# Own planned times for the first eight tiles of x, and whole projections copied to SBUF by ACT, in a hybrid attention block

## The chip, the cores and the metric

The kernel runs on one core of a Trainium2 chip. The metric is the device time of one execution in microseconds (us). Five engines work side by side, each through its own list of instructions, strictly in the order in which the program wrote them: PE (matmuls; PEld is its weight load), DVE (vector), ACT (activation), POOL, and SP, which here only issues DMAs. An instruction whose input is not there yet holds up everything behind it on its engine. Matmul results land in PSUM, in banks of 128x512 fp32.

## The reference, cut to what matters

```python
h = rms_norm(x, norm_gain)                      # x: 2048 x 1024, fp32
proj = h @ w_in                                 # q, k, v of mixers A and B; gates ga, gb; merge logits mg
qa = head_rms_norm(qa, q_norm_a) * scale;  ka = head_rms_norm(ka, k_norm_a)
ya, _ = banded_attention(qa, ka, va, A_WINDOW, 1, bias_a, sink_a)
ya = ya * silu(ga)
for g, (window, dilation) in enumerate(((128, 1), (512, 4), (2048, 16))):
    o, l = dilated_group(qb[:, :, g], kb[:, :, g], vb[:, :, g], window, dilation, bias_b[g])
yb = sum(softmax(stack(lses)) * stack(outs)) * silu(gb)
merged = sigmoid(mg_a + b) * (ya @ w_branch_a) + sigmoid(mg_b + b) * (yb @ w_branch_b)
y = x + merged @ w_out
```

## The kernel before

Precision comes from splitting: each fp32 operand of a matmul is a high and a low fp16 part, and a product is three matmuls (high by high, high by low, low by high). XH and XL are the parts of the normalised x, turned so that features lie on partitions; they stay in SBUF. A step named `hi` is ACT's conversion to fp16, a step `lo` is DVE's remainder after it.

There are three stages in time.

**Input stage.** x comes in 16 tiles of 128 rows, named t0 to t15 here. Each goes through: load (SP), sum of squares on ACT (L448), for a group of tiles together a first guess of 1/rms on DVE (L452, L261) and three Newton steps (12 small operations on POOL, L270 to L273, for groups of four; 9 on DVE, L275 to L277, for groups of two), a scaling on DVE (L462), then for each half of the features four transposes on PE (L468) into one of three PSUM banks "s", XH by ACT (L471) and XL by DVE (L475). T(t,h) is the group of four transposes of tile t, half h. The groups of tiles are (0,1), (2,3), (4..7), (8..11), (12..15). Beside this run projections of the gates: for gate block c (0 or 1) and quarter q of the rows (four tiles) a stream of 24 matmuls at L308, called c0q0, c1q0, c0q1 and so on. c0q0 needs tiles 0 to 3, and the split weights gh, gl of its block (raw weights graw, gain on POOL, norm, L350 and L354). At the start `warm` issues matmuls on constants.

**Units.** 14 units (a mixer's head group) of 8 pairs. A pair is two blocks of 128 rows: for each, the projection to q, k and v (24 matmuls at L651, or 48 where the rows of v are shifted against those of q and k) into one of two PSUM banks "pj". ACT copies q and k to the fp32 tile rw (evac_qk, L670), makes V's high part (v_hi, L685) from the same bank, DVE its low part (v_lo, L691). Then q and k are normalised: square (L698), sums and guess (L703, L704, L261), Newton on POOL, scale on DVE (L715), gain on POOL (L722), hi (L728), lo (L732), swap (L737), and a transposing DMA from SP (turn, L745) into kq, from which PE makes the logits (L805). Maxima (L820), exponentials (L828), their hi and lo (L833, L837), a turn (L843) and the values (L854) follow. Into eight units more gate projections are mixed, with a weight preparation: square of the raw gate weights on ACT (L332, which also gives gsq), and a small norm matmul on PE (L194).

**Tail.** Gates, branch projections, merge and output projection, nearly all of it PE work.

What sets the order is a table of numbers: a step is put into a heap with a planned time (`at(t, f)`, `chain` for steps that must follow each other), and `until(pos)` writes out all steps due before PE's planned position. These numbers decide the order of instructions and nothing else; on the chip only order, data and free buffers count. In the units time is counted in pairs: EVAC holds the delays of evac_qk, v_hi and v_lo after a projection, NORM those of the nine steps of the norm.

## Time and profile before

| | us |
|---|---|
| median of 3 runs (1957.21 to 1961.2) | 1960.59 |
| the profiled execution | 1960.34 |
| its span in the trace | 1958.6 |
| PE busy | 1935.7 |
| DVE busy | 1377.4 |
| ACT busy | 1059.8 |
| POOL busy | 956.0 |

The span runs from the first to the last recorded instruction; the time is 1.74 us longer than it. The input stage ends at about 81 us (first matmul of a unit's projection), the units at about 1449 us. A row of the timeline gives start, duration, engine, line, operation, output and inputs, and in brackets the idle time of the engine just before with what ended it. Matmuls are pipelined: the distance from one start to the next is what one costs, not its listed duration.

### The profile page before, as it was taken

The page shows a single profiled execution, that of the slowest core. Times are in us where ns is not written, and L with a number is a line of the kernel's source. Part 1 is how long each engine was busy: PE and PEld are TensorE (multiplying, and loading weights), DVE is VectorE, ACT ScalarE, POOL GpSimd, SP SyncE. Part 2 cuts the span into 40 slices and gives each one's busy share as a digit, 9 for nine tenths or more (in the row PEclk, how much of TensorE's full clock was granted, in tenths as well). Part 3 has the DMA queues.
Part 4 walks back from the last instruction along what each step waited for, and adds up shares of the span by engine and source line. Part 5 has one row for each costly group of instructions (what it writes and reads, how often), then busy time and mean ns, then how long its engine had stood idle before and what let it go on. Part 6 is the DMA issues. An engine that isn't in the chain of part 4 may idle for free.

```text
span 1958.6 us, 48091 instructions
## 1 busy us (share of the span) xinstructions
PE 1935.7 (99%) x17606; PEld 1392.0 (71%) x17606; DVE 1377.4 (70%) x3604; ACT 1059.8 (54%) x2415; POOL 956.0 (49%) x2440
## 2 busy tenths in 40 slices
PE   8999999999999999999999999999999999999999
PEld 5567896677788898888989889899544444444444
DVE  6668777888768776667876878767776757876312
ACT  7457656776565566565666655656534545432100
POOL 4254556455546656647566676656511210232533
PEclk8999999999999999999999999999999999999999
DMA  6239987797848596677777776755822346788763
GB/s 250 81 81 168 194 150 159 141 187 141 177 101 184 118 185 126 125 148 164 152 132 154 135 169 126 143 118 118 187 81 85 106 165 195 218 241 268 252 228 145
DMA packets 589773, 308.46 MB, mean 157 GB/s; under 512 B 458080, under 2 KB 527328, under 8 KB 588256
## 3 DMA queue, kind: packets, MB, share of 16 engines
q1 hardware_dynamic: 589536, 305.39, 67.0%
q8 instruction: 137, 2.24, 0.5%
q14 instruction: 100, 0.82, 0.1%
HBM read 129.91 MB, written 65.27 MB: 100 GB/s over the span
## 4 chain that ended last, share of the span: by engine, by line
PE 80%; DVE 6%; POOL 6%; issue 4%; ACT 2%; DMA 2%; SPq 0%; POOLq 0%; DVEq 0%; ACTq 0%
PE pj L651 32%; PE pj L308 14%; PE fps L308 13%; PE fps L1614 7%; PE fps L1409 5%; PE s L805 4%; PE pv L854 4%; POOL rs_t L270 1%; DVE rw L715 1%; POOL rs_t L271 1%; DVE qss L703 1%; POOL rs_t L272 1%; POOL rw L722 1%; POOL rs_y L273 1%; PE pt L916 1%
## 5 line engine op out<-in xcount | busy, mean ns | idle before, releaser
L651 PE MATMUL pj<-wl,XH 128*128 128x128 f16 (+2 forms) x2816 | 715.2, 268 | 0.0
L651 PE MATMUL pj<-wh,XH 128*128 128x128 f16 (+2 forms) x2816 | 708.7, 268 | 4.0 <-DVE vt L691 4.0
L651 PE MATMUL pj<-wh,XL 128*128 128x128 f16 (+2 forms) x2816 | 711.6, 269 | 0.0
L651 PEld LDWEIGHTS <-XH 128*128 128x128 f16 x5632 | 574.6, 113 | 64.7 <-issue 5.8
L651 PEld LDWEIGHTS <-XL 128*128 128x128 f16 x2816 | 318.1, 113 | 26.7 <-issue 0.5
L820 DVE CUSTOM_DVE_ANT_0 pr<-s,b,ubuf 128x256 f32<-128x256 f32 (+3 forms) x512 | 218.6, 464 | 48.6 <-PE s L805 47.0
L270 POOL TENSOR_TENSOR rs_t<-rs_y 128x8 f32<-128x8 f32 (+2 forms) x345 | 105.4, 306 | 207.5 <-DVE rs_y L261 142.7
L837 DVE SCALAR_TENSOR_TENSOR p<-pr,p 128x512 f16<-128x512 f32 (+2 forms) x256 | 185.0, 723 | 21.6 <-ACT p L833 21.1
L308 PEld LDWEIGHTS <-wh 128*128 128x128 f16 x960 | 93.7, 98 | 111.0 <-issue 1.5
L715 DVE TENSOR_TENSOR rw<-rw,qr 128x512 f32<-128x512 f32 (+1 forms) x112 | 111.6, 997 | 86.7 <-POOL vt L678 58.4
L722 POOL TENSOR_TENSOR rw<-rw,g 128x128 f32<-128x128 f32 (+1 forms) x224 | 131.1, 605 | 78.1 <-DVE rw L715 62.1
L833 ACT ACTIVATE p<-pr 128x512 f16<-128x512 f32 (+2 forms) x256 | 159.5, 623 | 7.1 <-issue 0.3
L670 ACT ACTIVATE rw<-pj 128x256 f32<-128x256 f32 (+1 forms) x224 | 86.5, 386 | 134.3 <-PE pj L651 133.4
L737 POOL COPY spl<-spl 128x256 f16<-128x256 f16 (+1 forms) x224 | 93.7, 448 | 127.2 <-DVE spl L732 125.7
L308 PE MATMUL fps<-Y,wh 128*128 128x512 f16 x512 | 152.2, 379 | 0.0
L805 PE MATMUL s<-kq 128*128 128x128 f16 (+1 forms) x1856 | 147.3, 218 | 1.5 <-DMA kq<-spl 1.4
L805 PEld LDWEIGHTS <-kq 128*128 128x128 f16 x2016 | 129.8, 98 | 25.1 <-issue 2.0
L308 PE MATMUL pj<-XH,gh 128*128 128x512 f16 x384 | 145.5, 379 | 0.0
L308 PE MATMUL pj<-XH,gl 128*128 128x512 f16 x384 | 145.5, 379 | 0.0
L308 PE MATMUL pj<-XL,gh 128*128 128x512 f16 x384 | 145.5, 379 | 0.0
L1614 PE MATMUL fps<-wt,M 128*128 128x512 f16 (+1 forms) x684 | 145.2, 375 | 0.0
L728 ACT ACTIVATE spl<-rw 128x512 f16<-128x512 f32 (+1 forms) x112 | 72.1, 644 | 126.2 <-POOL vt L678 87.0
(241 smaller groups left out, 3702.2 us busy)
## 6 DMA issues: line engine op xcount, KB each, us to landing
wraw<-in_w_units_dram SPq DMA_DIRECT2D x56, 384.0 KB, 4.6
mtd<-mm SPq DMA_DIRECT2D x56, 256.0 KB, 3.7
M<-mtd SPq DMA_DIRECT2D x8, 1792.0 KB, 9.5
mgd<-fg SPq DMA_DIRECT2D x39, 256.0 KB, 2.1
zd<-z SPq DMA_DIRECT2D x128, 66.0 KB, 1.9
zz<-zd SPq DMA_DIRECT2D x64, 132.0 KB, 2.9
xt<-in_x_dram SPq DMA_DIRECT2D x16, 512.0 KB, 8.9
gtd<-yo SPq DMA_DIRECT2D x32, 256.0 KB, 2.7
```

The costliest lines, as they stand in the source:

```text
L270: G.tensor_tensor(tv, yv, yv, OP.mult)
L308: out.append(lambda w=w, xx=xx, ch=ch, i=i: T.matmul(ps[:], lhsT=w[:, ch, c0:c0 + 128], rhs=xx[:, ch, ts], start=(i == 0), stop=(i == n - 1)))
L651: out.append(lambda lhs=lhs, rhs=rhs, ch=ch, a=a, b=b, k=k: T.matmul(ps[:, a:b], lhsT=lhs[:, ch, :], rhs=rhs[:, ch, a:b], start=(k == 0), ...
L715: V.tensor_tensor(q, q, self.rr[:, :n].unsqueeze(2).to_broadcast([128, n, HD]), OP.mult)
L722: G.tensor_tensor(q[:, i, :un.nq, :], q[:, i, :un.nq, :], g, OP.mult)
L737: G.tensor_copy(sp[:, i, nh:, :, :], sp[:, i, nq:nh, ::-1, :])
L805: T.matmul(self.sv[j][:, o:o + k1 - k0], lhsT=q[:, h, :], rhs=kt[:, un.nq + kh + v * un.nk, k0:k1], start=(v == 0), stop=(v == 1))
L820: V.tensor_tensor_reduce(out=self.pv[:, j, self.p0:self.p0 + W], in0=self.sv[j], in1=un.bias[:, self.h0 + j, self.b0:self.b0 + W], scale=I ...
L833: A.activation(self.sp[:, :128 * n], self.pr, AF.Copy, scale=PSC)
L837: V.scalar_tensor_tensor(self.sp[:, 128 * n:], self.pr, PSC, self.sp[:, :128 * n], OP.mult, OP.subtract)
L1409: mm.append(lambda ch=ch, k=k, w=w, i=i: T.matmul(ps[:], lhsT=weight(bl, ch)[w], rhs=xblock(x, ch)[k], start=(i == 0), stop=(i == 11)))
L1614: mm.append(lambda ch=ch, k=k, w=w, i=i: T.matmul(ps[:, :cols.stop - cols.start], lhsT=m[:, a, ch, k, :], rhs=wt[w][:, b, ch, cols], start ...
```

## The change

Input stage: the tables now give each of the first eight squares and scales, and each half tile of the first four tiles, a planned time of its own. The groups become (0,1), (2,3), (4,5), (6,7), (8..11), (12..15). The transposes of (1,1) and (2,0) go to the two "pj" banks. Warm matmuls are 60 at the start and 0, 6, 12, 8 later (24, 16, 16, 16, 12 before). A second copy of the first columns of XH and XL (x_again, POOL) moves from the start of the stage to its end, and a gate stream waits until its weights are planned to be ready.

Units: ACT copies all 384 columns of a projection to rw, and v_hi and v_lo read V from that copy instead of from PSUM. The planned times of v_hi and v_lo, and some others, are later. Lines of the changed program are 9 to 16 higher than those of the program before.

```diff
-EVAC = (0.015, 0.025, 0.099)
-NORM = (0.028, 0.136, 0.32, 0.626, 0.744, 0.904, 0.962, 1.033, 1.118)
+EVAC = (0.015, 0.04, 0.16)
+NORM = (0.028, 0.136, 0.295, 0.626, 0.744, 0.904, 0.962, 1.033, 1.118)
-LAGS = {'A': (...), 'B': (-0.156, -0.001, 0.042, 0.169, 0.19, 0.379, 0.525)}
+LAGS = {'A': (...), 'B': (-0.156, -0.001, 0.042, 0.152, 0.173, 0.362, 0.508)}
-A_MERGE = (0.085, 0.258, 0.51, 0.671, 1.503, 0.761)
+A_MERGE = (0.085, 0.1, 0.51, 0.671, 1.503, 0.761)
-GATE = (-0.123, -0.064, 0.329)
+GATE = (-0.123, 0.026, 0.419)
-G_PREP = (5.907, 6.882, 7.102, 7.671, 7.712, 7.812, 7.942)
+G_PREP = (5.907, 6.882, 7.04, 7.76, 7.8, 7.9, 8.03)
...
-X_WARM = (24, 16, 16, 16, 12)
+X_SQ = (4.7, 6.0, 7.67, 9.519, 13.423, 20.123, 22.646, 24.708, 27.708, 1.508)
+X_SC = (9.358, 10.138, 12.938, 13.688, 24.438, 25.089, 28.349, 29.268, 39.768, 2.218)
+X_NW = (7.25, 10.067, 20.868, 26.596, 36.596, 45.765)
...
+X_WARM = (60, 0, 6, 12, 8)
...
-    groups = {0: (0, 1), 1: (0, 1), 2: (2, 3), 3: (2, 3)}
-    groups.update((t, tuple(range(t - t % 4, t - t % 4 + 4))) for t in range(4, NT))
+    GROUPS = (0, 1), (2, 3), (4, 5), (6, 7), (8, 9, 10, 11), (12, 13, 14, 15)
...
-        rs_newton(ss, y, xss[g][:, :len(g)], len(g), len(g) > 2)
+        rs_newton(ss, y, xss[g][:, :len(g)], len(g), g[0] > 2)
...
+        k = 2 * t + h
+        ps = pj_p.tile([128, 512], F32, name="pj") if k in (3, 4) else s_p.tile([128, 512], F32, name="s")
...
         def evac_qk(self, i):
             if i == 0:
-                self.rw = wk.tile([128, 640], F32, name="rw")
-            n = self.nh * HD
-            A.activation(self.rw[:, n * i:n * i + n], self.ps[i][:, :n], AF.Copy)
+                self.rw = wk.tile([128, 2, 384], F32, name="rw")
+                self.q = self.rw[:, :, :self.nh * HD].rearrange("p s (h e) -> p s h e", e=HD)
+            A.activation(self.rw[:, i, :], self.ps[i][:, :384], AF.Copy)
...
-            psv = self.ps[i][:, w:w + nv * HD].rearrange("p (h e) -> p h e", e=HD)
+            psv = self.rw[:, i, w:w + nv * HD].rearrange("p (h e) -> p h e", e=HD)
             A.activation(vt[:, :nv, 0:HD], psv, AF.Copy, scale=VSC)
```

Three places show what the tables make of the order. The first is PE's list in the input stage, at tiles 9 to 12. In the rows of before, xt_170 is tile 9 and each "s" a PSUM bank; between two halves stand six matmuls of a gate stream, of which three are shown.

```order
L468 MATMUL s_643<-idf_73,xt_170 128x128 x4
L308 LDWEIGHTS gh_290
L308 MATMUL pj_605<-XH_80,gh_290 128x512
L308 LDWEIGHTS gh_290
L308 MATMUL pj_605<-XL_81,gh_290 128x512
L308 LDWEIGHTS gl_291
L308 MATMUL pj_605<-XH_80,gl_291 128x512
...
L468 MATMUL s_657<-idf_73,xt_170 128x128 x4
```

After, xt_231 is tile 9, xt_233 tile 10, xt_235 tile 11 and xt_237 tile 12; pj_773 is the stream c0q2.

```order
L479 MATMUL s_700<-idf_73,xt_231 128x128 x4
L479 MATMUL s_709<-idf_73,xt_233 128x128 x4
L479 MATMUL s_721<-idf_73,xt_233 128x128 x4
L479 MATMUL s_729<-idf_73,xt_235 128x128 x4
L479 MATMUL s_753<-idf_73,xt_235 128x128 x4
L479 MATMUL s_761<-idf_73,xt_237 128x128 x4
L317 LDWEIGHTS gh_310
L317 MATMUL pj_773<-XH_80,gh_310 128x512
L479 MATMUL s_775<-idf_73,xt_237 128x128 x4
```

Six half tiles now stand in a row, with no gate matmul between them, ahead of c0q2. The streams before that place carry fewer: c0q1 carries none at all.

The second place is DVE's list at the same point of the changed program, from the stats of tiles 12 to 15 (xss_592) to the scale of tile 12; yo is the product of a gate.

```order
L461 TENSOR_SCALAR xss_592<-xss_592 128x4
L270 TENSOR_SCALAR rs_y_715<-xss_592 128x4
L387 SCALAR_TENSOR_TENSOR yo_705<-yo_705,pj_645 128x512
L486 TENSOR_TENSOR XL_81<-s_700,XH_80 128x4x128
L471 TENSOR_SCALAR xt_235<-xt_235,xr_629 128x1024
L486 TENSOR_TENSOR XL_81<-s_709,XH_80 128x4x128
L486 TENSOR_TENSOR XL_81<-s_721,XH_80 128x4x128
L471 TENSOR_SCALAR xt_237<-xt_237,xr_734 128x1024
L486 TENSOR_TENSOR XL_81<-s_729,XH_80 128x4x128
```

The scale of tile 12, on which the sixth of these half tiles waits, stands behind the low parts of tile 10 and takes its factor xr_734 from the Newton steps of the last group. In the list of before the scale of tile 12 also stands right behind the low parts of tile 10; what moved is PE's side, where T(12,0) has no gate matmuls in front of it any more.

The third place is in the units: ACT's list at the last block of a pair in unit 10, with the square of the raw gate weights behind it. Before:

```order
L670 ACTIVATE rw_15565<-pj_15561 128x256
L685 ACTIVATE vt_15660<-pj_15561 128x2x64
L698 ACTIVATE spl_15679<-rw_15565 128x512
L828 ACTIVATE pr_15621<-pr_15621,nmB_14085 128x256 x2
L997 ACTIVATE bm_e_15617<-bm_e_15617 128x12
L833 ACTIVATE p2_15689<-pr_15621 128x512
L332 ACTIVATE gh_15694,gsq_15696<-wraw_15429 128x1024
```

After:

```order
L686 ACTIVATE rw_15585<-pj_15581 128x384
L714 ACTIVATE spl_15698<-rw_15585 128x512
L841 ACTIVATE pr_15641<-pr_15641,nmB_14104 128x256 x2
L341 ACTIVATE gh_15703,gsq_15705<-wraw_15465 128x1024
L701 ACTIVATE vt_15680<-rw_15585 128x2x64
L1010 ACTIVATE bm_e_15637<-bm_e_15637 128x12
L846 ACTIVATE p2_15711<-pr_15641 128x512
```

Square and exponentials now come ahead of v_hi, and the square of the gate weights moves two places forward. On PE the first matmul of the next projection into the same bank changes what it waits for. Before, then after:

```order
L651 MATMUL pj_15673<-wh_13113,XL_81 128x256
L651 LDWEIGHTS XH_80
L651 MATMUL pj_15800<-wh_13113,XH_80 128x128 [waits DVE_49]
L651 LDWEIGHTS XH_80
L651 MATMUL pj_15800<-wl_13114,XH_80 128x128
```

After:

```order
L667 MATMUL pj_15693<-wh_13135,XL_81 128x256
L667 LDWEIGHTS XH_80
L667 MATMUL pj_15820<-wh_13135,XH_80 128x128 [waits Activation_49]
L667 LDWEIGHTS XH_80
L667 MATMUL pj_15820<-wl_13136,XH_80 128x128
```

The bank was released by DVE's v_lo, and is now released by ACT's copy. Transposes of halves (1,1) and (2,0), warm matmuls and the place of the gate weights' norm matmul (some 40 rows later in PE's list, about 20 matmuls) also moved; the rest of PE's list is in the same order.

More of the change, by code (lines that the diff above doesn't have):

```diff
@@ L126, in block_kernel @@
     sm = main.enter_context(tc.tile_pool(name="sm", bufs=4))
-    ubuf = us.tile([128, 192], F32, name="ubuf")
+    ubuf = us.tile([128, 168], F32, name="ubuf")
     ucount = [0]
@@ L258, in rs_guess @@
     def rs_guess(a, n):
-        y = sm.tile([128, 10], F32, name="rs_y")
+        y = sm.tile([128, 10], F32, name="rs_y", bufs=3)
         V.tensor_scalar(y[:, :n].bitcast(I32), a.bitcast(I32), -0.5, float(0x5F3759DF), OP.mult, OP.add)
@@ L264, in rs_newton @@
     def rs_newton(a, yv, r, n, pool):
-        t = sm.tile([128, 10], F32, name="rs_t")
+        t = sm.tile([128, 10], F32, name="rs_t", bufs=3)
         tv = t[:, :n]
@@ L437, in small_scales @@
         V.tensor_scalar(bmh[:], bmt[:], 0.5, None, OP.mult)
-    groups = {0: (0, 1), 1: (0, 1), 2: (2, 3), 3: (2, 3)}
-    groups.update((t, tuple(range(t - t % 4, t - t % 4 + 4))) for t in range(4, NT))
+    GROUPS = (0, 1), (2, 3), (4, 5), (6, 7), (8, 9, 10, 11), (12, 13, 14, 15)
+    groups = {t: g for g in GROUPS for t in g}
     def x_square(t):
@@ L464, in x_turn @@
     def x_turn(t, h):
-        xps[t, h] = ps = s_p.tile([128, 4, 128], F32, name="s")
+        k = 2 * t + h
+        ps = pj_p.tile([128, 512], F32, name="pj") if k in (3, 4) else s_p.tile([128, 512], F32, name="s")
+        xps[t, h] = ps = ps[:].rearrange("p (a b) -> p a b", a=4)
         for c in range(4):
@@ L512, in scale_time @@
     def scale_time(t):
-        return X_CH[0] + X_CH[1] * t
+        return X_SC[t] if t < 8 else X_SC[8] + X_SC[9] * (t - 8)
     def ready_time(t):
-        return scale_time(t) + sum(X_CH[2:])
-    for t, n in enumerate(X_WARM):
-        at(scale_time(t) + X_CH[2] - .05 if t < 4 else scale_time(3) + X_CH[2] + X_CH[5] + .05, warm, n)
-    for t in range(NT):
-        b = X_SQ[0] + X_SQ[1] * t if t < 4 else X_SQ[2] + X_SQ[3] * (t - 4)
-        at(b, x_square, t)
-        if t == groups[t][-1]:
-            at(b + X_ST[0], x_stats, groups[t])
-            at(b + X_ST[0] + X_ST[1], x_newton, groups[t])
+        return X_LO[2 * t + 1] if t < 4 else scale_time(t) + sum(X_CH)
+    for t, n in zip(X_WT, X_WARM):
+        at(t, warm, n)
+    for k, g in enumerate(GROUPS):
+        at(X_NW[k], x_stats, g)
+        at(X_NW[k] + X_ST, x_newton, g)
+    for t in range(NT):
+        at(X_SQ[t] if t < 8 else X_SQ[8] + X_SQ[9] * (t - 8), x_square, t)
         b = scale_time(t)
@@ L528, in block_kernel @@
         for h in range(2):
-            b = scale_time(t) + X_CH[2] + X_CH[5] * h
-            at(b, x_turn, t, h)
-            at(b + X_CH[3], x_hi, t, h)
-            at(b + X_CH[3] + X_CH[4], x_lo, t, h)
+            if t < 4:
+                tu, hi, lo = (v[2 * t + h] for v in (X_TU, X_HI, X_LO))
+            else:
+                tu = b + X_CH[0] + X_CH[3] * h
+                hi = tu + X_CH[1]
+                lo = hi + X_CH[2]
+            at(tu, x_turn, t, h)
+            at(hi, x_hi, t, h)
+            at(lo, x_lo, t, h)
         if t < 2:
             for k in range(2):
-                at(ready_time(t) + 1.0 + 1.2 * k, x_again, t, (XH, XL)[k])
+                at(X_AGAIN + 4 * t + 2 * k, x_again, t, (XH, XL)[k])
         if t + XT_BUFS < NT:
-            at(ready_time(t), x_load, t + XT_BUFS)
-    for c in range(3):
-        b = X_G[c]
+            at(ready_time(t) + .05, x_load, t + XT_BUFS)
+    for c, ts in enumerate((X_G0, X_G1, X_G2)):
         if c == 2:
-            at(X_G[0] + X_GP[5] + .1, g_load, c)
-        chain([(b + X_GP[0] * i, g_gain, c, i) for i in range(2)]
-              + [(b + d, f, c) for d, f in zip(X_GP[1:], (g_square, g_sum, g_pow, g_hi, g_lo))])
+            at(X_G0[5] + .1, g_load, c)
+        chain([(ts[0] + X_GD * i, g_gain, c, i) for i in range(2)]
+              + [(b, f, c) for b, f in zip(ts[1:], (g_square, g_sum, g_pow, g_hi, g_lo))])
     at(X_W[0], w_load, 0)
@@ L697, in square @@
             self.sq = self.sp[:].rearrange("p a b c d -> p (a b c d)").bitcast(F32)
-            A.activation(self.sq[:, :n], self.rw[:, :n], AF.Square)
+            A.activation(self.sq[:, :n].rearrange("p (s a) -> p s a", s=2), self.rw[:, :, :n // 2], AF.Square)
         def stats(self):
             n = 2 * self.nh
-            ss = sm.tile([128, 10], F32, name="qss")
+            ss = sm.tile([128, 10], F32, name="qss", bufs=3)
             V.tensor_reduce(ss[:, :n], self.sq[:, :n * HD].rearrange("p (h e) -> p h e", e=HD), AX.X, OP.add)
```

43 lines of the change are left out of this document (24 added, 19 removed).

## The prediction

> **What bounds the kernel now.** I read the page's busy times first, then busy time by stage, then PE's waits, then the timeline at the places where PE waits. The page:
>
> ```profile
> PE 1935.7 (99%) x17606; PEld 1392.0 (71%) x17606; DVE 1377.4 (70%) x3604; ACT 1059.8 (54%) x2415; POOL 956.0 (49%) x2440
> ```
>
> PE is the bound, so only PE's gaps can be won, or new ones opened. By stage (start and end, length, then busy time of PE, PEld, DVE, ACT, POOL, granted clock, DMA share):
>
> ```profile
> 28.00:81.00 53.00, 52.87 (x297) 30.79 (x298) 41.97 (x96) 34.69 (x60) 15.41 (x32) 1.00 0.18 68
> 81.00:1449.00 1368.00, 1357.66 (x14834) 1115.98 (x14833) 1020.92 (x3003) 827.18 (x2032) 787.63 (x2276) 1.00 0.73 146
> 1449.00:1958.60 509.60, 505.95 (x2360) 230.80 (x2358) 298.32 (x463) 178.48 (x290) 140.30 (x106) 1.00 0.57 187
> ```
>
> From 28 us on the input stage is full. In the units PE lacks some 10 us of 1368, and the tail is not touched by the change. PE's waits (total, times, longest):
>
> ```profile
> PE s L468 <- DVE xt L462: 6.4, 4, 4.7
> PE pj L651 <- DVE vt L691: 4.0, 4, 2.4
> ```
>
> The first row is the start, where tiles are late; the second is the wait for V's low part, which the change takes away. Those are the two places.
>
> **Input stage.** The rows that price it: DVE's guess and nine Newton steps (first and last), a scale, two low parts, a gate's low part; then PE's T(4,0), a later half tile with two gate matmuls, and the first unit matmul.
>
> ```profile
> 12.03 0.96 DVE L261 TENSOR_SCALAR rs_y<-xss 128x2 int32<-128x2 int32 x1
> 13.03 0.16 DVE L275 TENSOR_TENSOR rs_t<-rs_y 128x2 f32<-128x2 f32 x1
> 14.59 0.16 DVE L277 SCALAR_TENSOR_TENSOR xr<-rs_t,rs_y 128x2 f32<-128x2 f32 x1
> 14.67 0.75 DVE L462 TENSOR_SCALAR xt<-xt,xr 128x1024 f32<-128x1024 f32 x1
> 23.50 1.28 DVE L475 TENSOR_TENSOR XL<-s,XH 128x512 f16<-128x512 f32 x2
> 22.30 1.28 DVE L354 SCALAR_TENSOR_TENSOR gl<-graw,ubuf,gh 128x1024 f16<-128x1024 f32 x1
> 28.13 0.63 PE L468 MATMUL s<-idf,xt 128*128 128x128 f32 x4 [0.48 <-DVE xt L462]
> 57.09 0.60 PE L468 MATMUL s<-idf,xt 128*128 128x128 f32 x4
> 57.53 0.38 PE L308 MATMUL pj<-XH,gh 128*128 128x512 f16 x1
> 57.74 0.38 PE L308 MATMUL pj<-XL,gh 128*128 128x512 f16 x1
> 80.63 0.33 PE L651 MATMUL pj<-wh,XH 128*128 128x384 f16 x1
> ```
>
> A half tile costs PE 0.44 (57.09 to 57.53), a gate matmul 0.217. What stands in PE's list from T(4,0) on takes 80.63 - 28.13 = 52.5 us of before, without a gap worth naming. The changed list has the same work (192 gate matmuls, 24 half tiles) from its first gate matmul on, in another order. So the end of the stage is that first matmul, plus 52.5, plus new waits.
>
> The first matmul: the guess of tiles 2 and 3 ends at 13.0 as before. On DVE follow the scale of t1 (0.7, to 13.75), nine Newton steps (1.75, to 15.5), the scales of t2 and t3 (17.0), two low parts (0.65 each, 18.3), the seven small steps of the gate norm (0.19 each as in Newton, 19.6), the other four low parts up to tile 3 that stand ahead of gl (22.15), gl (1.2 to the next start, 23.35). PE's warm matmuls are over at about 22.9, and its third gate matmul needs gl: it starts at 22.95. Then the stage could end at 22.95 + 52.5 = 75.45, a lead of 5.2 us.
>
> I expect the lead to be spent, because tiles 4 to 12 do not come earlier by as much. Prices: the twelve Newton steps on POOL (first and last), scales beside POOL's work, a gate product.
>
> ```profile
> 43.82 0.20 POOL L270 TENSOR_TENSOR rs_t<-rs_y 128x4 f32<-128x4 f32 x1 [5.59 <-DVE rs_y L261]
> 47.40 0.20 POOL L273 TENSOR_TENSOR xr<-rs_t,rs_y 128x4 f32<-128x4 f32 x1
> 48.57 1.00 DVE L462 TENSOR_SCALAR xt<-xt,xr 128x1024 f32<-128x1024 f32 x1
> 26.50 1.49 DVE L462 TENSOR_SCALAR xt<-xt,xr 128x1024 f32<-128x1024 f32 x1 [1.72 <-POOL xr L273]
> 57.36 0.69 DVE L378 SCALAR_TENSOR_TENSOR yo<-yo,pj 128x512 f32<-128x512 f32 x1
> ```
>
> Newton on POOL is 3.8 with its gaps; I take 3.4 to 3.8, and a scale at 0.75 to 1.0. Carried through the four lists by hand (estimates):
> - T(4,0): ACT finishes the square of t5 at 22.55, stats to 23.55, Newton to 27.25, scale to 28.0. PE asks at 27.5 (21 gate matmuls): wait 0.5.
> - T(6,0): the second square after that, stats at 30.3, Newton to 33.75, scale to 34.75. PE asks at 28.0 + 18 x 0.217 + 4 x 0.44 = 33.7: wait 1.05, with the turn to it 1.2.
> - T(8,0): the stats of tiles 8 to 11 stand behind the low part of T(7,1), at 41.5; Newton to 45.3, scale to 46.4. PE asks at 34.9 + 42 x 0.217 + 4 x 0.44 = 45.8: wait 0.55.
> - The six half tiles in a row: PE comes at 51.0 and has 2.6 us of work there. T(12,0), the sixth, waits for DVE: from 45.4 five scales (3.9), six low parts (3.9), two gate products (1.4), stats (0.35) and 1.2 of waits for ACT and POOL, so 56.15. PE is through at 56.7, not 53.7: wait 3.0.
> - c0q2 then meets low parts of tile 11 and one late scale: 0.6.
>
> Together 5.85: the first unit matmul comes at 81.3, +0.7 against 80.63. To this comes the clock. These windows show PE's busy time and, after five engines, the granted clock:
>
> ```profile
> 21.15:24.56 3.41, 1.66 (x14) 1.13 (x12) 3.38 (x6) 3.41 (x7) 2.70 (x6) 1.00 1.06 391
> 24.57:27.98 3.41, 3.08 (x15) 1.86 (x13) 1.70 (x3) 1.90 (x5) 2.37 (x8) 0.50 1.02 384
> 1120.24:1123.66 3.42, 1.11 (x17) 0.93 (x16) 3.30 (x12) 2.56 (x7) 1.33 (x4) 1.00 0.32 89
> 1123.66:1127.07 3.41, 3.30 (x29) 2.87 (x30) 2.44 (x11) 3.12 (x9) 2.54 (x11) 0.50 0.77 156
> ```
>
> Twice a window with PE half idle or more is followed by one at half clock. The six half tiles give such a window (under half busy); at half clock the next would lose some 1.0 to 1.7 us. I add half of 1.2, since the windows may fall otherwise. **Input term: +0.7 + 0.6 = +1.3**, between -5.2 (no wait) and about +6 (rival b). The Trainium skill ("TensorE: Matmul & The Clock Gate", "What's actually happening") puts the half clock behind an idle window of about 3.4 us. By that rule read strictly a half-busy window would cost nothing and the sum would be 0.6 lower; the two pairs of rows above go against so strict a reading.
>
> The 60 first warm matmuls lie under the wait for x, where no one waits for PE; without that cover they would cost their own time. The x_again copies on POOL, moved to the end of the stage, cost nothing while POOL has 15 of 53 us busy.
>
> **Units.** The largest of the four waits for V's low part:
>
> ```profile
> 1119.17 0.37 ACT L670 ACTIVATE rw<-pj 128x256 f32<-128x256 f32 x1
> 1119.70 0.27 PE L651 MATMUL pj<-wh,XL 128*128 128x256 f16 x1
> 1121.10 0.91 ACT L828 ACTIVATE pr<-pr,nmB 128x256 f32<-128x256 f32 x2 [0.89 <-DVE nmB L820]
> 1121.40 0.68 DVE L732 TENSOR_TENSOR spl<-rw,spl 128x512 f16<-128x512 f32 x1
> 1122.33 0.22 PE L651 MATMUL pj<-wh,XH 128*128 128x128 f16 x1 [2.36 <-DVE vt L691]
> 1122.58 1.04 ACT L332 ACTIVATE gh<-wraw 128x1024 f16<-128x1024 f32 x1
> 1123.77 0.58 PE L194 MATMUL pt<-gsq,ones 128*128 128x1 f32 x2 [0.33 <-ACT gh L332]
> ```
>
> ACT had copied the bank by 1119.54, before PE wanted it; the low part stood on DVE behind the maxima and L732. With the copy of all columns the bank is free at once. Start to start PE loses 2.5 us here, 0.35 at the gsq matmul (L194), and 0.95 in the half clock behind (its window, 1123.66 on, is 3.41 us; some 1.9 of it are projection matmuls at twice their distance, which loses half; an estimate). The other waits of the 4.0 us, by window, the first row 1070 to 1140, the others 1360 to 1400:
>
> ```profile
> PE pj L651 <- DVE vt L691: 2.8, 2, 2.4
> ...
> PE pj L651 <- DVE vt L691: 0.8, 1, 0.8
> PE s L805 <- DMA kq<-spl: 0.8, 1, 0.8
> ```
>
> The second of the first row is 0.4, the one outside both windows 0.4 too; with PE's refilling 0.6 and 0.5, so 4.9 in all. The wait of 0.8 has a wait for kq of the same size near it, which then takes its place: nothing. Two new waits are to be paid: PE now reaches the gsq matmul at about 1122, while L332 cannot start before the exponentials end at 1122.0 and takes 1.2, so 1.25; and the logits behind come 0.25 before their kq (an estimate). **Unit term: -4.9 + 1.5 = -3.4**, between 0 (all turns into other waits) and -6.7 (nothing does).
>
> What the copy costs, by form of the copy:
>
> ```profile
> L670 ACT ACTIVATE rw<-pj 128x256 f32<-128x256 f32 x192 | 72.8, 379 | 114.5 <-PE pj L651 114.0 <-DVE spl L732 0.2
> L670 ACT ACTIVATE rw<-pj 128x320 f32<-128x320 f32 x32 | 13.8, 430 | 19.8 <-PE pj L651 19.4 <-DVE spl L732 0.4
> ```
>
> 64 columns are 51 ns, so 384 columns 481 ns: 192 x 0.102 + 32 x 0.051 = 21 us more on ACT, which is 54% busy; the square stands ahead of v_hi now, and that gives the norm chain back what the copy takes. I cost it at 0; if ACT ran out, kq would be late next. V's low part, now with both inputs in SBUF:
>
> ```profile
> L691 DVE SCALAR_TENSOR_TENSOR vt<-pj,vt x204: 210/284/294, 85.3 to 1382.6; 128x128 f16<-128x128 f32 x86, 128x64 f16<-128x64 f32 x16
> L715 DVE TENSOR_TENSOR rw<-rw,qr x112: 679/796/2109, 94.7 to 1387.9; 128x512 f32<-128x512 f32 x96, 128x640 f32<-128x640 f32 x16
> ```
>
> From PSUM it never stretched (210 to 294 ns); the scale with SBUF inputs does, by 0.12 in the median over its least and by 1.4 at most. I take 0, since nobody on PE waits for it any more. The Trainium skill ("SBUF — State Buffer", "Who interferes with whom") says that a DVE instruction with two SBUF inputs and a POOL instruction that reads SBUF shut each other out for a whole instruction, which speaks against this change. The trace agrees as to L715; with 0.12 at the two places where kq decides, the sum would be 0.24 higher.
>
> **Sum**, on the profiled execution (0.25 under the median of the runs): 1960.34 + 1.3 - 3.4 = 1958.2. A difference under 0.2% (3.9 us) can't be told from no change, so this is "same": faster begins under 1956.7, slower over 1964.5.
>
> **Rivals.**
> a) The lead of the input stage is kept. If the six half tiles cost only their 2.6 us and the clock stays, the units start at 78.3: -2.3 - 3.4, 1954.6; with all waits gone, at 75.45: 1951.7. For it: five of the waits rest on my carrying four lists by hand. Against: each of the four squares, guesses and Newtons stands in a row.
> b) Slower: DVE and POOL get into each other's way at the six half tiles. Five scales at 1.49 (the 26.50 row) instead of 0.8 are 3.5, and a Newton stretched with them 1.5: units start at 86.3, 1960.3 + 5.7 - 3.4 = 1962.6. From a start at 84.0 on the change as a whole loses, from 88 on measurably.
> c) The bank is free earlier and nothing comes of it: kq or gsq takes over every gap, 1960.3 + 1.3 = 1961.6. For it: at the fourth place that is what I expect.
>
> **Chances.** Forecast 0.45 (1956 to 1960.5), a 0.24, b 0.17, c 0.14. Faster: most of a and a quarter of the forecast, less what noise returns: 0.36. Slower: the upper part of b and some of c: 0.14. Same: 0.50. Range: 1952.0, inside a, to 1964.5, over b.
>
> **What the profile after would show.** The first gate matmul at 23 us, where T(4,0) came at 28.13; a wait of about 3 us on the scale of tile 12 near 54 us, and the first unit matmul at 81.3. No PE wait for V's part; in unit 10 a wait for gsq of about 1.2 us and no half clock there; ACT's copy near 480 ns. I am wrong if the units start before 79 or after 84, or if waits for kq grow by more than 2 us.

## The result and the profile after

The changed kernel takes 1972.23 us (median of three, 1970.23 to 1972.73) against 1960.59: a ratio of 1.0060 [1.0046, 1.0074], so it is 0.6% slower, clear of the noise, and above the range of the prediction. A second measurement on another chip gave 1967.28 against 1959.49, 1.0037 [1.0025, 1.0050]. The profiled execution took 1972.23, with a span of 1970.5 against 1958.6. First the busy times on the page, then busy time by stage (columns as for before):

```profile
PE 1935.0 (98%) x17608; PEld 1391.3 (71%) x17608; DVE 1392.3 (71%) x3606; ACT 1088.5 (55%) x2415; POOL 973.7 (49%) x2452
```

```profile
28.00:85.40 57.40, 50.94 (x272) 29.32 (x271) 43.06 (x89) 35.17 (x62) 21.10 (x48) 0.94 0.17 63
85.40:1459.70 1374.30, 1355.14 (x14835) 1114.33 (x14834) 1034.23 (x3000) 856.58 (x2032) 806.57 (x2276) 1.00 0.69 145
1459.70:1970.50 510.80, 506.32 (x2360) 230.77 (x2359) 297.80 (x466) 178.14 (x290) 138.88 (x106) 1.00 0.57 186
```

PE is busy as long as before (1935.0 for 1935.7), so in sum the loss is idle time of PE: 57.40 - 50.94 = 6.5 us of it in the input stage, where before had 0.1, and 19.2 in the units, where before had 10.3. The stages end 4.75, 10.8 and 11.9 us later than before: input stage +4.75, units +6.1, tail +1.1. In a second profile of the changed kernel (after_again below) it is +3.9, +3.5 and -0.3, so the first of these holds better than the other two. PE's waits (total, times, longest):

```profile
PE s L479 <- DVE xt L471: 8.8, 5, 2.3
PE s L818 <- DMA kq<-spl: 7.4, 7, 2.2
PE pt L203 <- DVE yo L933: 4.9, 2, 2.6
PE pj L667 <- ACT rw L686: 1.9, 2, 1.5
PE pt L203 <- ACT gh L341: 1.7, 2, 1.1
PE pt L929 <- DVE wm L210: 1.5, 2, 1.2
```

The wait for V's low part is gone altogether. In its place stand small waits for many things: kq (1.4 before), the copy itself, gsq, a norm of the gate weights (wm). Waits for yo, a gate product, are 4.9 in all, 3.0 before. That list is the answer in short; the rest of this document finds out why.

**The input stage.** The first gate matmul, the four places at which PE waits for a scaled tile, and the first unit matmul:

```profile
23.06 0.38 PE L317 MATMUL pj<-XH,gh 128*128 128x512 f16 x1
35.22 0.63 PE L479 MATMUL s<-idf,xt 128*128 128x128 f32 x4 [1.61 <-DVE xt L471]
47.41 0.63 PE L479 MATMUL s<-idf,xt 128*128 128x128 f32 x4 [1.19 <-DVE xt L471]
55.01 1.16 PE L479 MATMUL s<-idf,xt 128*128 128x128 f32 x8 [1.55 <-DVE xt L471]
58.29 1.09 PE L479 MATMUL s<-idf,xt 128*128 128x128 f32 x4 [2.12 <-DVE xt L471]
85.38 0.33 PE L667 MATMUL pj<-wh,XH 128*128 128x384 f16 x1
```

The lead of 5 us is there at 23.06 and spent by 58.29. What makes the tiles late is seen on DVE and POOL, here at tiles 6 and 12; tile 8, at 45.33, looks like tile 6:

```profile
33.06 1.47 POOL L189 TENSOR_TENSOR wraw<-wraw,gn 128x768 f32<-128x768 f32 x1
33.14 1.93 DVE L471 TENSOR_SCALAR xt<-xt,xr 128x1024 f32<-128x1024 f32 x1 [1.54 <-POOL xr L282]
56.56 1.04 POOL L333 TENSOR_TENSOR graw<-graw,gn 128x512 f32<-128x512 f32 x1
56.64 1.50 DVE L471 TENSOR_SCALAR xt<-xt,xr 128x1024 f32<-128x1024 f32 x1 [0.58 <-POOL xr L282]
```

Each time POOL's last Newton step releases two things in the same instant: DVE's scale, and the next instruction in POOL's own list, a gain over a whole piece of weights. POOL starts 0.08 us earlier, and the scale ends 0.54 us after the gain, both times: 1.93 and 1.50 us instead of 0.75. So the coincidence is no accident of this execution; the Newton steps themselves bring it about.

Then the clock. In the trace it changes only at the ends of windows of 3.41 us. PE alone by these windows: PE busy, granted clock, DMA share, GB/s:

```profile
49.89:53.30 3.41, 3.41 (x25) 1.00 0.00 0
53.30:56.71 3.41, 1.33 (x10) 1.00 0.21 79
56.71:60.13 3.42, 1.84 (x8) 0.50 0.00 0
60.13:63.54 3.41, 3.41 (x13) 0.50 0.00 0
```

Behind a window in which PE was busy 39%, the clock is at half for two windows, from 56.71 to 63.54. PE works in them from 58.29 to 63.44, a gate matmul every 0.427 us instead of 0.216, so 5.15 us do the work of 2.6 and 2.5 are lost. In the second profile only one window is at half (58.32 to 61.73), and the units start 0.84 us earlier.

**The units.** The start of the same PE instruction in both profiles shows where the lag grows (us):

| place | before | after | lag |
|---|---|---|---|
| first unit matmul | 80.63 | 85.38 | 4.75 |
| after a wait for the gate product yo | 290.06 | 296.76 | 6.70 |
| same, a later unit | 512.01 | 517.93 | 5.92 |
| behind a half clock that only before has here | 516.04 | 520.31 | 4.27 |
| end of unit 9, logits wait for kq | 995.02 | 1001.52 | 6.50 |
| unit 10, weight sum waits for ACT wl | 1082.59 | 1089.91 | 7.32 |
| unit 10, logits wait for kq | 1113.61 | 1122.18 | 8.56 |
| V wait gone | 1122.33 | 1128.37 | 6.04 |
| half clock gone, gsq waited for | 1125.78 | 1131.12 | 5.33 |
| wm and ACT's copy waited for | 1134.72 | 1141.59 | 6.86 |
| unit 12, wm, gsq | 1379.15 | 1388.46 | 9.30 |
| unit 13, kq | 1398.71 | 1409.52 | 10.81 |
| first matmul of the tail | 1448.90 | 1459.71 | 10.81 |

Three things happen. At the gate product PE waits 2.6 us at 296.76, where before did not wait; at the next one before waits 3.0 us itself and then runs at half clock, so the lag falls to 4.27. From unit 9 to the middle of unit 10 the lag grows by 2 us through waits for the norm chain's outputs. And the gains at V waits are handed back: in unit 10, 4.6 us are gained at the V wait and the half clock behind it, start to start, and 2.9 are paid again by 1141.59; in unit 12, 1.6 are gained and 2.8 paid.

### The profile page after: what moved, and what is told of

Read it like the earlier page. It is cut to its first block, busy times and chain, and to the rows that moved or that the text cites. A ratio compares the mean times of both kernels' runs of the same rounds, so it can differ in the third digit from the quotient of the medians.

```text
span 1970.5 us, 47899 instructions
## 1 busy us (share of the span) xinstructions
PE 1935.0 (98%) x17608; PEld 1391.3 (71%) x17608; DVE 1392.3 (71%) x3606; ACT 1088.5 (55%) x2415; POOL 973.7 (49%) x2452
## 5 line engine op out<-in xcount | busy, mean ns | idle before, releaser
L667 PEld LDWEIGHTS <-XH 128*128 128x128 f16 x5632 | 575.1, 113 | 61.3 <-issue 2.2
L850 DVE SCALAR_TENSOR_TENSOR p<-pr,p 128x512 f16<-128x512 f32 (+2 forms) x256 | 190.3, 743 | 16.7 <-ACT p L846 15.8
L279 POOL TENSOR_TENSOR rs_t<-rs_y 128x8 f32<-128x8 f32 (+3 forms) x348 | 92.5, 266 | 207.1 <-DVE rs_y L270 178.3
L737 POOL TENSOR_TENSOR rw<-rw,g 128x128 f32<-128x128 f32 (+1 forms) x224 | 137.7, 635 | 75.3 <-DVE rw L731 60.3
L686 ACT ACTIVATE rw<-pj 128x384 f32<-128x384 f32 x224 | 108.3, 483 | 107.5 <-PE pj L667 105.7
L750 POOL COPY spl<-spl 128x256 f16<-128x256 f16 (+1 forms) x224 | 101.8, 484 | 126.2 <-DVE spl L745 124.5
```

The costliest lines, as they stand in the source:

```text
L279: G.tensor_tensor(tv, yv, yv, OP.mult)
L667: out.append(lambda lhs=lhs, rhs=rhs, ch=ch, a=a, b=b, k=k: T.matmul(ps[:, a:b], lhsT=lhs[:, ch, :], rhs=rhs[:, ch, a:b], start=(k == 0), ...
L686: A.activation(self.rw[:, i, :], self.ps[i][:, :384], AF.Copy)
L737: G.tensor_tensor(q[:, i, :un.nq, :], q[:, i, :un.nq, :], g, OP.mult)
L750: G.tensor_copy(sp[:, i, nh:, :, :], sp[:, i, nq:nh, ::-1, :])
L850: V.scalar_tensor_tensor(self.sp[:, 128 * n:], self.pr, PSC, self.sp[:, :128 * n], OP.mult, OP.subtract)
```

## The experiments

All times are against the kernel before on the same chip; a ratio's interval is 95%. A single profile scatters by some 3 us (the waits for kq above all), so profiles are used for the waits at fixed places, and the timings for totals.

**Which half costs.** The changed kernel again; the changed kernel with the input stage of before (units_only); the kernel before with the changed input stage alone (input_only).

> The changed kernel once more, for a second profile. If the waits of the units come from the order of the instructions, the same waits stand at the same places with the same length (kq 1.6 us near 1001, 2.4 near 1122, 2.4 near 1409; ACT's copy 1.7 near 1141; gsq 1.3 near 1380). If they come from transfers that land at other times in each execution, the kq waits move by a microsecond or more and others take their place. Time 1970 to 1973 us in both cases.

> The changed kernel with the input stage of before (its tables, groups, warm matmuls and functions); the units and the tail as changed. After the change the first unit matmul came 4.75 us later, the units took 6.1 us longer and the tail 1.1 us. Theory 1 (the two losses are separate, each made by its own part): first unit matmul at 80.6 as before, time about 1960.5 + 6 + 1 = 1967.5 us. Theory 2 (the units lose because the late input stage shifts their transfers): units as fast as before or faster, 1957 to 1961 us.

> The kernel before with the changed input stage; units and tail as before. Theory 1: first unit matmul at 85.4, units as before, about 1960.5 + 4.7 = 1965 us. Theory 2: the shifted units lose here too, 1970 us or more.

| | ratio | us (ratio - 1, of 1960) | units start | units' length |
|---|---|---|---|---|
| after_again | 1.0037 [1.0025, 1.0050] | +7.3 | 84.54 | 1371.78 |
| units_only | 1.0030 [1.0019, 1.0040] | +5.9 | 81.58 | 1373.45 |
| input_only | 1.0010 [1.0002, 1.0019] | +2.0 | 84.94 | 1365.33 |

Both halves lose, the units most; within the intervals the two add up to the whole. The units of the program before, started 4.3 us later, are 2.9 us shorter in this profile (1365.33 for 1368.27). All of that lies at 512 to 516 us, where the lag falls from 4.3 to 1.3: there the profile of before has its wait of 3.0 us for yo and the half clock, and this one a wait of 1.7 and no half clock.

The wait of 2.6 us for yo at 296.76 comes from the units' half too, and with the changed gate rows of the tables: at that matmul six of the seven profiles that have these rows wait 1.4 to 2.6 us (the seventh 0.3), and those with the old rows at most 0.6, but for two kernels that are over 2% slower throughout (vlo_early and best2 below).

**The scale behind the gain.** In no_gain six gains on POOL are left out: those of the first unit's weights (four) and of the last gate block in the input stage (two); that part of the result isn't computed.

```diff
+        if u == 0:
+            return          # w_gain
...
+        if c == 2:
+            return          # g_gain
```

> The changed kernel with six POOL instructions left out of the input stage: the gain on the weights of unit 0 (four) and on the third block of gate weights (two); so these weights lack their gain. Order otherwise the same. Theory A (DVE's scales are shut out by POOL's gains): the scales of tiles 6, 8, 9, 12 fall from 1.93, 1.93, 1.35 and 1.50 to about 0.75 us, the first unit matmul comes about 3 us earlier (82.4), and the time falls by as much, to about 1969 us. Theory B (the six half tiles in a row and the chain of squares, guesses and Newton steps set the time of the stage, whatever POOL does): under 1 us earlier.

```profile
43.42 0.75 DVE L475 TENSOR_SCALAR xt<-xt,xr 128x1024 f32<-128x1024 f32 x1 [3.40 <-POOL xr L284]
53.45 1.04 POOL L494 COPY XH<-XH 128x1024 f16<-128x1024 f16 x1
53.55 1.49 DVE L475 TENSOR_SCALAR xt<-xt,xr 128x1024 f32<-128x1024 f32 x1 [0.57 <-POOL xr L284]
82.66 0.33 PE L671 MATMUL pj<-wh,XH 128*128 128x384 f16 x1
```

The scales of tiles 6, 8 and 9 now take 0.75 us. That of tile 12 does not, against what was expected: it stays at 1.49, because the x_again copy (L494), next in POOL's list, has taken the gain's place and is released together with the scale just as the gain was. The mean of all 16 scales falls from 1046 to 829 ns. The units start at 82.66: 2.7 earlier than in the first profile of the changed kernel, 1.9 earlier than in the second. Part of that was there before any of these scales: from the first gate matmul to the first unit matmul it is 60.3 us here and 62.3 and 61.3 in those two.

So the mechanism is shown, for the copy as for the gain; its worth at tiles 6, 8 and 9 is some 1.0 to 2.0 us at the start of the units. The kernel's time, 1.0029 [1.0018, 1.0040], can't be told from after_again's.

**The half clock.** In warm_burst 12 and 18 matmuls on constants fill PE's waits ahead of tiles 11 and 12.

```diff
+    for t, n in ((47.0, 12), (49.0, 18)):
+        at(t, warm, n)
```

> The changed kernel with 12 matmuls on constants ahead of T(11,0) and 18 ahead of T(12,0), which fill the two waits among the six half tiles in a row. After the change PE ran 5.8 us at half clock behind these waits and lost 2.9 us. If the clock follows PE's idle time in the windows ahead, the half clock goes: first unit matmul 2.5 to 3 us earlier (81.7 to 82.2), time 2 us lower than the changed kernel's. If the half clock has another cause: no change.

```profile
51.80:55.20 3.40, 3.16 (x27) 1.00 0.20 75
55.20:58.60 3.40, 3.25 (x28) 1.00 0.02 4
```

With PE 93 and 96% busy around these waits the clock stays at full speed, behind them too, and the units start at 83.35, 1.2 to 2.0 us earlier than in the two profiles of the changed kernel (the warm matmuls take time of their own). The whole took 1.0046 [1.0034, 1.0059]: nothing of it is seen at the end.

**What a late start is worth.** In delay_only the kernel before gets 40 matmuls on constants late in the input stage, 4.3 us of pure delay.

```diff
+    at(56.0, warm, 40)
```

> The kernel before with 40 matmuls on constants (4.3 us of PE) put between two gate matmuls late in the input stage: a pure delay. The first unit matmul comes 4.3 us later. If lateness is partly taken back in the units (PE's wait for a transfer near 512 us and the half clock behind it, 3.2 and 1.6 us, need not come later with it): 1.5 to 3 us slower, as input_only (2.5). If lateness goes through: 4.3 us slower.

The units start at 84.36 (+3.7), and the time is 1.0021 [1.0012, 1.0029], +2.3 to +5.7 us. The units are 2.6 us shorter in the profile, and 1.1 of that lies at the same place, 512 to 516 us; the timing doesn't show as much taken back. Between input_only (+0.4 to +3.7 for 4.3 put in) and this run the share that comes back, none or half, stays open. So a microsecond or two at the start, as in no_gain and warm_burst, can't be read off at the end.

**Copy or tables.** copy_only is the kernel before with the wide copy and V from the copy (and the shorter buffer rings that come with them in the change), with the old tables; tables_only is the kernel before with the new unit tables and V still from PSUM; old_gate is units_only with the two rows of the table for gate preparation put back.

```diff
 copy_only
-            A.activation(self.rw[:, n * i:n * i + n], self.ps[i][:, :n], AF.Copy)
+            A.activation(self.rw[:, i, :], self.ps[i][:, :384], AF.Copy)
-            psv = self.ps[i][:, w:w + nv * HD]...
+            psv = self.rw[:, i, w:w + nv * HD]...
 tables_only
-EVAC = (0.015, 0.025, 0.099)
+EVAC = (0.015, 0.04, 0.16)
 ... (and NORM, LAGS, B_LAST, DRAIN, A_MERGE, GATE, G_PREP of the change)
 old_gate
-GATE = (-0.123, 0.026, 0.419)
-G_PREP = (5.907, 6.882, 7.04, 7.76, 7.8, 7.9, 8.03)
+GATE = (-0.123, -0.064, 0.329)
+G_PREP = (5.907, 6.882, 7.102, 7.671, 7.712, 7.812, 7.942)
```

> The kernel before with one part of the change: ACT copies all 384 columns and V's parts read the copy; all tables as before, so V's high part stands right behind the copy again. Prediction's own term (waits for V's low part go, little comes in their place): 3 to 4 us faster than before, 1956. Rival (ACT's longer copy and the low part with two SBUF inputs lengthen the loop copy, square, Newton, gain, hi, next copy by 0.2 to 0.4 us a pair where it decides): same as before or up to 3 us slower.

> The kernel before with the changed tables of the units (EVAC, NORM, LAGS, B_LAST, DRAIN, A_MERGE, GATE, G_PREP) and V's parts still read from PSUM. If the tables make the loss, it is there without the copy, and larger, since V's later low part now holds the PSUM bank: 1968 us or more. If the copy makes it: 1960 to 1963.

> The kernel with the input stage of before and the units as changed (units_only, 5.3 us slower than before), with two tables put back: GATE and G_PREP, the times of the gate steps and of the preparation of the gate weights. Theory 1 (the later norm of the gate weights holds ACT: its conversion of the gate weights waits for DVE's norm, and the copy of the projection stands behind it): the waits for gsq (0.8 to 1.5 us near 1125 and 1375), for wm (0.7 and 1.3) and for ACT's copy (0.7 and 1.1) go, some 4 us; time 1960 to 1961. Theory 2 (the loss comes from the V parts and the longer copy): no change against units_only, 1964 to 1965.

copy_only 1.0031 [1.0020, 1.0043], tables_only 1.0072 [1.0059, 1.0085], old_gate 1.0013 [1.0005, 1.0022]. PE's waits in tables_only, then in copy_only:

```profile
PE pj L651 <- DVE vt L691: 14.9, 17, 3.1
```

```profile
PE pt L194 <- ACT gh L332: 7.0, 3, 3.0
```

Later tables need the copy: with V's low part read late from PSUM the bank is held in 17 places. The copy under the old tables takes every V wait away, and gets a wait for gsq of 3.0 instead where the largest V wait, 2.4, had been; in unit 12 another of 3.0 stands where a V wait of 0.8 was, and with the half clock behind it the lag grows there from 3.8 to 9.1. old_gate has the same wait; PE reaches that matmul while ACT still has exponentials to do:

```profile
1124.25 0.38 PE L194 MATMUL pt<-gsq,ones 128*128 128x1 f32 x2 [2.82 <-ACT gh L332]
```

In the changed kernel the tables put the square (L341) earlier and that matmul later, and the wait at it is only 0.53. The rest turns up behind:

```profile
1130.87 0.38 PE L203 MATMUL pt<-gsq,ones 128*128 128x1 f32 x2 [0.53 <-ACT gh L341]
...
1135.98 0.70 DVE L707 SCALAR_TENSOR_TENSOR vt<-rw,vt 128x128 f16<-128x128 f32 x1
...
1138.76 0.66 PE L929 MATMUL pt<-idf,ya 128*128 128x128 f32 x4 [0.38 <-DVE wm L210]
...
1139.49 1.15 ACT L359 ACTIVATE gh<-wraw,ubuf 128x1024 f16<-128x1024 f32 x1 [3.04 <-DVE ubuf L217]
...
1141.07 0.47 ACT L686 ACTIVATE rw<-pj 128x384 f32<-128x384 f32 x1
1141.59 0.22 PE L667 MATMUL pj<-wh,XH 128*128 128x128 f16 x1 [1.52 <-ACT rw L686]
```

The norm of the gate weights (L210, at 1138.56) now stands behind V's low part and three more instructions on DVE; ACT sits 3.04 us before L359 for it; the copy that frees PE's bank is queued behind L359. Read upward from the last row, that is PE waiting for a copy that waits for a conversion that waits for a norm. 0.53 + 0.38 + 1.52 comes to 2.4 us, as much as the V wait had cost, in three pieces. With the gate rows put back (old_gate) the second and third piece are gone.

**Who delays kq.** Behind a projection, the pair loop is: copy, square (ACT), sums (DVE), Newton (POOL), scale (DVE), gain (POOL), hi (ACT), and hi stands ahead of the next pair's copy on ACT. Where this loop is PE's limit (units 9 and 10, and 12 and 13), a step that gets longer by a little is paid once for each pair. From the second copy of pair 76 to that of pair 84, eight pairs, before needs 72.2 us (1025.86 to 1098.06) and after 74.0 (1031.95 to 1105.93). The steps from scale to hi in one of these pairs, before and then after:

```profile
1085.42 0.69 DVE L715 TENSOR_TENSOR rw<-rw,qr 128x512 f32<-128x512 f32 x1 [2.34 <-POOL vt L678]
1086.03 0.68 DVE L837 SCALAR_TENSOR_TENSOR p<-pr,p 128x512 f16<-128x512 f32 x1
1086.26 1.18 POOL L722 TENSOR_TENSOR rw<-rw,g 128x128 f32<-128x128 f32 x2 [0.83 <-DVE rw L715]
1087.47 0.63 ACT L728 ACTIVATE spl<-rw 128x512 f16<-128x512 f32 x1 [3.20 <-POOL vt L678]
```

```profile
1092.72 0.69 DVE L731 TENSOR_TENSOR rw<-rw,qr 128x512 f32<-128x512 f32 x1 [2.26 <-POOL vt L694]
1093.33 0.29 DVE L707 SCALAR_TENSOR_TENSOR vt<-rw,vt 128x128 f16<-128x128 f32 x1
1093.54 0.69 DVE L850 SCALAR_TENSOR_TENSOR p<-pr,p 128x512 f16<-128x512 f32 x1
1093.56 1.39 POOL L737 TENSOR_TENSOR rw<-rw,g 128x128 f32<-128x128 f32 x2 [0.83 <-DVE rw L731]
1094.99 0.63 ACT L741 ACTIVATE spl<-rw 128x512 f16<-128x512 f32 x1 [3.15 <-POOL vt L694]
```

Before, the low part of the exponentials (L837) has been running for 0.23 us when POOL's gain starts. After, V's low part (L707) goes in between, so L850 and the gain start 0.02 us apart, and the gain takes 1.39 instead of 1.18: in the mean over these pairs 0.20 us more from gain to hi. The wider copy adds 0.085 from copy to square. Together that is 0.29 us a pair; from the square to the scale it is 0.06 less, so 0.22 us remain, or 1.8 over eight pairs if every one of them is bound by the loop. 1.8 were found.

This was tested by moving V's low part alone: vlo_early puts it back to its old planned time, vlo_late behind that of L850 (both from old_gate; only DVE's list differs).

```diff
 vlo_early
-EVAC = (0.015, 0.04, 0.16)
+EVAC = (0.015, 0.04, 0.099)
 vlo_late
+EVAC = (0.015, 0.04, 0.25)
```

> The kernel of old_gate (input stage of before, changed units, old tables for gate steps and gate weights) with one number put back: V's low part is planned 0.099 pairs after its projection instead of 0.16, so that on DVE it no longer stands between the scale of a pair and the low part of the probabilities (L850). In the changed order ACT's copy falls 0.29 us per pair further behind in units 9 and 12, of which 0.20 lies between POOL's gain and ACT's hi. Theory 1 (V's low part delays L850, and POOL's gain then waits for it): gain to hi is back at the time of before, the copy falls behind by under 0.12 us a pair, waits for kq and for the weight norm shrink by 2 us in all, time 1 to 3 us under old_gate's, about that of before. Theory 2 (it is ACT's copy with its 0.10 us more): no change, 0.13% slower than before like old_gate.

> The kernel of old_gate (0.13% over before) with one number changed: V's low part planned 0.25 pairs after its projection instead of 0.16. Only DVE's list changes: the low part of V no longer stands between the scale of q and k and the low part of the probabilities (L850) but behind it, and it does not move ahead of the stats, which is what made vlo_early slow. In old_gate the time from POOL's gain to ACT's hi was 0.20 us a pair longer in units 9 and 12, and from ACT's copy to the square 0.085. Theory 1 (V's low part delays L850, and POOL's gain waits until L850 lets go): gain to hi falls back to that of before, ACT's copy falls behind by 0.09 us a pair instead of 0.29, and the time is 1 to 3 us under old_gate's. Theory 2 (the longer copy, or something else that changes with it, makes the gain late): no change in gain to hi.

vlo_early: 1.0229 [1.0215, 1.0243], 44 us slower. vlo_late: 1.0002 [0.9991, 1.0012]. DVE's waits in vlo_early:

```profile
DVE vt L691 <- ACT vt L685: 163.5, 163, 3.9
```

V's high part now comes late on ACT, behind the square; with V's low part ahead of the sums on DVE, the sums wait for it too and come 1.0 us later behind the square in these eight pairs. That spoiled it as a test of the gain, but it shows that the loop is the limit: 44 us over 112 pairs is 0.4 us a pair, and in the eight pairs above 8.6 us are lost. vlo_late is the clean test:

```profile
1082.18 0.69 DVE L715 TENSOR_TENSOR rw<-rw,qr 128x512 f32<-128x512 f32 x1 [2.34 <-POOL vt L678]
1082.79 0.69 DVE L834 SCALAR_TENSOR_TENSOR p<-pr,p 128x512 f16<-128x512 f32 x1
1083.03 1.23 POOL L721 TENSOR_TENSOR rw<-rw,g 128x128 f32<-128x128 f32 x2 [0.83 <-DVE rw L715]
1083.39 0.55 DVE L691 SCALAR_TENSOR_TENSOR vt<-rw,vt 128x128 f16<-128x128 f32 x1
```

L834 follows the scale directly and the gain is back at 1.23 (from gain to hi 1.16 in the mean of the eight pairs; 1.23 before, 1.43 in old_gate); V's low part, which now takes the collision (0.55), has no one behind it that matters. Over the eight pairs the lag against before grows by 0.13 us, where old_gate's grew by 1.86, and the wait for ACT wl in unit 10 is gone.

copy_only fits the same loop by another step. There V's high part stands between copy and square, which come 0.30 us further apart, and from gain to hi nothing changes. The changes from copy to square, square to scale and gain to hi, summed and taken eight times, give 1.8 us for the changed kernel, 1.7 for copy_only, 0.1 for vlo_late and 8.6 for vlo_early; found are 1.8, 1.7, 0.1 and 8.6. The copy of the next pair follows hi by the same 0.54 us in all of them, so there is no slack, and in these pairs the loop alone sets the pace. From pair 100 to 108 (units 12 and 13) it is the same: 2.1, 2.2, 0.8 and 9.2, summed and found. From pair 92 to 100 the sums are 1.2 to 2.4 us larger than what is found: there the loop has slack.

In total, units_only, old_gate and vlo_late form a ladder: +5.9 (3.7 to 7.8), +2.5 (1.0 to 4.3; the gate rows put back) and +0.4 us (-1.8 to +2.4; V's low part out of the way). The intervals of neighbours overlap, and the runs were on three chips; by the times alone only the two ends are clear of each other.

**In search of something faster.** best1 is the kernel before (V from PSUM) with V's low part and the gate square earlier; best2 is vlo_early, best3 is vlo_late, each with that earlier square; after_vlo is the changed kernel with the later V low part.

```diff
 best1
-EVAC = (0.015, 0.025, 0.099)
+EVAC = (0.015, 0.025, 0.05)
 best1, best2, best3
-G_PREP = (5.907, 6.882, 7.102, ...)
+G_PREP = (5.907, 6.882, 7.04, ...)
 after_vlo
-EVAC = (0.015, 0.04, 0.16)
+EVAC = (0.015, 0.04, 0.25)
```

> The kernel before with V's parts still read from PSUM, V's low part planned earlier (0.05 instead of 0.099 pairs) and the square of the gate weights at 7.04. If the waits for V's low part come only from its place on DVE behind the low part of q and k (L732), it stands ahead of it now, PE's waits (4.0 us) go without any copy, and the time falls by 2 to 4 us; the gsq wait is again what can take the gain away.

> vlo_early with the square of the gate weights on ACT planned earlier (7.04 instead of 7.102 in G_PREP, as in the change), ahead of the next copy or exponentials. In old_gate PE waits 2.5 us for gsq at the two places where it waited for V's low part before. Theory 1: these two waits shrink by 1 to 1.5 us each; 2 to 3 us under vlo_early, the first version faster than before. Rival: the square then delays ACT's copy and the exponentials by as much, and the time stays.

> vlo_late with the square of the gate weights ahead of V's high part and of the scaling of the exponentials on ACT (G_PREP 7.04 instead of 7.102). In old_gate PE waited 2.5 us for gsq at each of two places. Expected: 1 us less at each, 1 to 2 us under vlo_late; with it the first version under the time of before (by 0 to 3 us).

> The changed kernel itself with V's low part planned 0.25 pairs after its projection. By theory 1 above 1 to 3 us under the changed kernel (0.37% over before on its second chip, so 0.22 to 0.32%), by theory 2 the same as it.

best1 1.0011 [1.0002, 1.0020]: V waits remain (4.6 us in six places), those for gsq are gone. best2 1.0268 [1.0254, 1.0282] shares vlo_early's fault. best3 0.9997 [0.9989, 1.0006]: its two large waits for gsq shrink from 2.87 to 2.08 and from 3.08 to 2.28, and no time is won (a wait of 0.66 for another of DVE's steps opens). after_vlo 1.0038 [1.0026, 1.0051], no better than after_again. Its profile shows the mechanism (the eight pairs take 72.3 us again, 73.8 in after_again) and is 2.2 us shorter, but the timing doesn't confirm it. So in the whole changed kernel V's place is shown to speed up the loop, and not to save time; nor do old_gate and vlo_late, whose intervals overlap, show by the times what it is worth. No version beat the kernel before.

## Why the prediction was wrong

**What bounds it**: right. PE is the bound in both, and nothing but its gaps and its clock changed.

**Input stage, forecast +1.3, found +4.75 (4.3 with the other unit code).** The first matmul was right (22.95, found 23.06), so was the place of each wait. The step that failed is "a scale at 0.75 to 1.0". Start to start PE lost nothing at T(4,0) (0.5 forecast), 1.77 at T(6,0) (1.2), 1.35 at T(8,0) (0.55), and 1.71 + 2.28 at the six half tiles (3.0); together 7.1 where 5.85 with c0q2's 0.6 was carried. The scales behind these waits took 1.93, 1.93 and 1.50 us. The price of 1.49 stood in a quoted row and was kept for rival b; it, or a longer one, is paid wherever in these traces Newton on POOL releases a scale while a long gain or copy follows in POOL's list, and that could have been read from POOL's order. Rival b gave 86.3 for the start of the units, 85.38 was measured, and it had a chance of 0.17. The second mis-sized term is the clock: 0.6 forecast, as half of 1.2, and 2.5 found (one window at half in the second profile, two in the first). The two windows quoted for it led to a half clock each time, and the window at the six half tiles was 34 to 39% busy and led to a half clock in all five profiles that have this input stage without warm_burst's matmuls, so halving it was the error. The Trainium skill ("TensorE: Matmul & The Clock Gate", "What's actually happening") asks for an idle window; here one in which PE was busy 39% was enough. What the input half cost at the end is 0.4 to 3.7 us, by input_only.

**Units, forecast -3.4, found +6.1 (+3.5 in the second profile).** The four V waits went and so did the half clock behind the largest, as said; the copy's 481 ns was right:

```profile
L686 ACT ACTIVATE rw<-pj 128x384 f32<-128x384 f32 x224 | 108.3, 483 | 107.5 <-PE pj L667 105.7
```

Two steps failed. The first is the price of what comes next, "so 1.25" for gsq. Copy_only and old_gate show that the whole 2.4 turns into a wait for gsq when the gate rows of the tables stay, and the changed tables, where gsq itself is only 0.53, spread it over wm and the copy; in unit 12 gsq (1.5) and wm (1.3) cost 2.8, where the V wait (1.0 with its refill) and a half clock (0.7) had cost 1.7. I looked one wait ahead, and the wait behind that one (DVE's norm, behind V's low part) was not in the sum. Rival c, that something else takes over every gap, is what happened at these places, and in unit 12 it cost more than the gap. The changed gate rows, with which PE waits for yo, had no term in the sum at all.

The second is "I cost it at 0" for the copy and "I take 0" for V's low part. The reason given was ACT's busy share of 54% and that nobody on PE waits for V's low part any more. Both are true and beside the point: ACT and DVE are in a loop that is PE's limit in some units, and it's the place in the loop that costs. V's low part didn't hurt by being slow but by delaying L850 into POOL's gain. Both signs that were to tell that the prediction is wrong came: the units start after 84, and the waits for kq grew by 6.0 us in the first profile and 2.1 in the second. By groups, POOL's gain in before, after and vlo_late:

```profile
L722 POOL TENSOR_TENSOR rw<-rw,g 128x128 f32<-128x128 f32 (+1 forms) x224 | 131.1, 605 | 78.1 <-DVE rw L715 62.1 <-DVE bm_d L1000 5.6 <-DVE am_n L953 4.8
```

```profile
L737 POOL TENSOR_TENSOR rw<-rw,g 128x128 f32<-128x128 f32 (+1 forms) x224 | 137.7, 635 | 75.3 <-DVE rw L731 60.3 <-DVE am_n L966 5.0 <-DVE bm_d L1013 3.7
```

```profile
L721 POOL TENSOR_TENSOR rw<-rw,g 128x128 f32<-128x128 f32 (+1 forms) x224 | 127.7, 590 | 78.2 <-DVE rw L715 61.1 <-DVE am_n L950 5.0 <-DVE bm_d L997 4.7
```

30 ns in the mean of 224 look like nothing; in the pairs that set PE's pace it was 0.2 us each. The rule weighed in the prediction ("SBUF — State Buffer", "Who interferes with whom" in the Trainium skill: a DVE instruction with two SBUF inputs and a POOL instruction that reads SBUF shut each other out) agrees with the rows of the pair above, where a gain that starts 0.02 us behind L850 takes 1.39 and one that starts 0.23 behind L837 takes 1.18. I priced it at 0.24 by the median stretch of the instruction itself, and not by who stands behind it.

**What stays open**: the tail, 1.1 us longer in the first profile, is 0.3 shorter in the second, so no lasting loss is shown there. The wait for kq in unit 10 (2.2 us at 1122.18) is 1.2 to 2.2 us in every profile with the copy and the new tables, 1.5 in vlo_late too, so V's place is not all of its cause, and what the rest is stays open. How much of a late start the units take back stays open too.
